# A transformer block on one core: another chain in its opening, three unread products instead of four, and one tensor for what a k-tile reads

## The chip, the core and the metric

The kernel runs on one core of one Trainium2 chip. Its engines work side by side: TensorE (PE) multiplies, with weight loads (PEld) that overlap its products; VectorE (DVE) and ScalarE (ACT) do elementwise work; GpSimd (POOL) and SyncE (SP) issue DMAs here, which 16 DMA engines carry out. The metric is the time of one execution in microseconds of the device (us).

## The reference

One block with 256 tokens of width 1024, all in float32. A vector c gives six modulation vectors; the tokens are scaled and shifted by two of them and multiplied by w_in. The opening of the kernel, which the change touches, computes this:

```
mod = jax.nn.silu(c) @ w_ada[l] + b_ada[l]
sh1, sc1, g1, sh2, sc2, g2 = jnp.split(mod[:, None, :], N_MOD, axis=-1)
h = x * (1.0 + sc1) + sh1
y = token_mixer(h, w_in[l], ...)          # begins with proj = h @ w_in
x = layer_norm(DEEPNORM_ALPHA * x + g1 * y, ln1_g[l], ln1_b[l])
...
y = conv_ffn(h, ...)
x = layer_norm(DEEPNORM_ALPHA * x + g2 * y, ln2_g[l], ln2_b[l])
```

The mixer is attention and a retention branch with gates; conv_ffn is a gated feed-forward layer with a convolution over three tokens. Both come after the opening and stay as they are.

## The kernel before

Products are made with split numbers: a float32 operand becomes a high part (a rounded copy that ACT writes) and a low part (the difference, which DVE writes), and three products stand for one: high by high, high by low, low by high. The helper `split` (L65 to L67) makes both parts, `mm3` (L80 to L83) the three products. ACT writes `whi` and DVE `wlo` for weights, `hh` and `hl` for tokens.

The opening works on eight k-tiles of 128 rows of the inner dimension, in an order written out by hand in `SEQ` (L34). For tile j:

- `a j`, in `h1(j, 0)` (L161): the load of ada tile j is read. DVE multiplies it with the row `srow` (silu of c, spread over all partitions by transposes on PE, L133 to L144) and sums along the row: two instructions of L153, one for the scale and one for the shift, and L170 adds the bias. This gives the modulation `mod` of tile j as two columns.
- `W j`, in `halves_A` (L181): the tile of 2048 columns of w_in is split in two halves of 1024. Behind the first piece of the first half the function `mid` is called, which is `h1(j, 1)`: ACT makes `h32`, the modulated tokens, from the transposed tokens `xT` with mod as scale and bias (L174); for j from 1 up `split` makes `hh` (a copy of h32) and `hl`. For j = 0 DVE makes `hh` straight from xT (L189), and ACT's h32 serves `hl` alone. Pieces are 512 wide in tile 0 (`j < CHUNK`).
- `P j`, in `products_A` (L196): 24 products of 512 columns into eight PSUM banks. In tile 0 they come in the order high by high for both token blocks, high by low for both, low by high for both (L204); in the others as three of `mm3` for each token block, so that `hl` is read by the third product.
- `X`/`Q` are two further weight tiles between them, for a gate.

Before the first real product PE executes `BUSY` products whose result nothing reads (L146 to L148), each on the first 512 columns of ada tile 0.

Loads are issued by SP in order (L70 to L75), into four buffers of 1 MB (`RAW_BUFS`); `load_A` (L114) issues the next of the list when a buffer has been read: for a weight tile first the tokens xT (128 KB) and then the weights (1 MB). `PIECES` says in how many pieces along the columns a tile is loaded: ada tile 0 in three, weight tiles 0 to 3 in four each, all others whole. In the instruction order a load waits for the completion of the load eight before it, and for the readers of its buffer. Ada tiles, tokens and weight tiles lie in three tensors, ada1, xT and winA, with rows of 8 KB, 1 KB and 8 KB, each k-tile a block without gaps.

After the opening the stream of the other weights and PE's products run on in an order fixed by the program; that code is not touched.

Of the kernel before, what the change touches and what calls it, by code (L numbers as in the profile page):

```python
# [9 lines left out]
AF = mybir.ActivationFunctionType  # L10
OP = mybir.AluOpType
# [16 lines left out]
CONST_AT, FIRST = 1, 2  # L28
T0_AT, XN, PRIME = 4, 256, 3
W0, W1, W2 = (4, 5), (6,), (7,)  # L30
PIECES = dict(ada1=[(0, 512, 1024, 2048)] + [1] * 7, winA=[4] * 4 + [1] * 4, winX=[1] * 2)
CHUNK = 1
BUSY = 4
SEQ = [(s[0], int(s[1])) for s in  # L34
       ("a0 W0 P0 a1 W1 P1 a2 W2 P2 a3 W3 P3 X0 Q0 a4 X1 W4 Q1 P4 a5 W5 P5 a6 W6 P6 a7 W7 P7").split()]

# [15 lines left out]
def _body(nc, a, out, pe, act, dve, sp, cst, wts, big, tmp, ps, dram):  # L52
    f = lambda ap: ap.bitcast(F32)
# [4 lines left out]
    def slot(n, shape, dt=F32):  # L58
        return big.tile(shape, dt, tag=f"A{n}", name=f"A{n}")
# [5 lines left out]
    def split(hi, lo, src):  # L65
        act.activation(hi, src, AF.Copy)  # L66
        dve.tensor_tensor(lo, src, f(hi), OP.subtract)  # L67


    def load_raw(src, pieces=1):  # L70
        t = wts.tile([128, 2048], F32, tag="raw", name="raw", bufs=RAW_BUFS)
        cuts = range(0, 2049, 2048 // pieces) if isinstance(pieces, int) else pieces
        for c0, c1 in zip(cuts, cuts[1:]):
            sp.dma_start(t[:, c0:c1], src[:, c0:c1])  # L74
        return t  # L75

    def new_hl():
        return [wts.tile([128, 1024], F32R, tag=n, name=n, bufs=HL_BUFS) for n in ("whi", "wlo")]

    def mm3(o, lh, ll, rh, rl, start, stop):  # L80
        pe.matmul(o, lh, rh, start=start, stop=False)  # L81
        pe.matmul(o, lh, rl, start=False, stop=False)  # L82
        pe.matmul(o, ll, rh, start=False, stop=stop)  # L83
# [19 lines left out]
    mod = cst.tile([128, 6, 8], F32, name="mod")  # L103

    raws = {}
# [8 lines left out]
    def load_A():  # L114
        if not loads_A:
            return
        name, j = loads_A.pop(0)
        if name == "winA":
            raws["xT", j] = slot(("3a", "3b", "6a", "6b")[j % 4], [128, 256])
            sp.dma_start(raws["xT", j], a["xT"][j])  # L120
        raws[name, j] = load_raw(a[name][j], PIECES[name][j])

    for _ in range(RAW_BUFS):
        load_A()
# [20 lines left out]

    for i in range(BUSY):  # L146
        raw = raws["ada1", 0]
        pe.matmul(bank(5), raw[:, i * 128:i * 128 + 128], raw[:, :512], start=True, stop=True)  # L148

    def ada(raw, sec, j, rows=slice(0, 1024)):  # L150

        junk = tmp.tile([128, 1024], mybir.dt.bfloat16, name="junk", bufs=1)
        dve.tensor_tensor_reduce(out=junk[:, rows], in0=raw[:, rows], in1=srow[:, rows], scale=1.0, scalar=0.0,  # L153
                                 op0=OP.mult, op1=OP.add, accum_out=mod[:, sec, j:j + 1])


    hh = slot(0, [128, 8, 256], F32R)
    hl = slot(1, [128, 8, 256], F32R)
    pa = [bank(i) for i in range(8)]

    def h1(j, part):  # L161

        if part == 0:
            ra = raws.pop(("ada1", j))
            if j == 0:
                ada(ra, 0, 0, slice(0, 512))
                dve.tensor_tensor(bcol[:, 0, 0:1], bcol[:, 0, 0:1], mod[:, 0, 0:1], OP.add)
            for i in range(2):
                ada(ra[:, i * 1024:(i + 1) * 1024], i, j, slice(512 if i == j == 0 else 0, 1024))
            dve.tensor_tensor(mod[:, 0:2, j], mod[:, 0:2, j], bcol[:, 0:2, j], OP.add)  # L170
            load_A()
        else:
            h32 = slot(("7a", "7b")[j % 2], [128, 256])
            act.activation(h32, raws.pop(("xT", j)), AF.Identity, scale=mod[:, 0, j:j + 1],  # L174
                           bias=mod[:, 1, j:j + 1])
            if j:
                split(hh[:, j], hl[:, j], h32)
            else:
                dve.tensor_tensor(hl[:, j], h32, f(hh[:, j]), OP.subtract)

    def halves_A(name, j, mid=lambda: None):  # L181
        rw = raws.pop((name, j))
        for half in range(2):
            hi, lo = whl[name, j, half] = new_hl()
            w = 512 if name == "winA" and j < CHUNK else 1024
            for c in range(0, 1024, w):
                if name == "winA" and j == half == c == 0:

                    dve.tensor_scalar(hh[:, 0], raws["xT", 0], mod[:, 0, 0:1], mod[:, 1, 0:1],  # L189
                                      op0=OP.mult, op1=OP.add)  # L190
                split(hi[:, c:c + w], lo[:, c:c + w], rw[:, half * 1024 + c:half * 1024 + c + w])
                if half == c == 0:
                    mid()
        load_A()

    def products_A(j):  # L196
        for half in range(2):
            hi, lo = whl.pop(("winA", j, half))
            for c in range(2):
                if j == 0:  # L200
                    cs = slice(c * 512, (c + 1) * 512)
                    for i, (x, w) in enumerate(((hh, hi), (hh, lo), (hl, hi))):
                        for t in range(2):
                            pe.matmul(pa[half * 4 + c * 2 + t], x[:, j, t * 128:(t + 1) * 128], w[:, cs],  # L204
                                      start=i == 0, stop=False)
                    continue
                for t in range(2):
                    mm3(pa[half * 4 + c * 2 + t], hh[:, j, t * 128:(t + 1) * 128],
                        hl[:, j, t * 128:(t + 1) * 128], hi[:, c * 512:(c + 1) * 512],
                        lo[:, c * 512:(c + 1) * 512], j == 0 or j == 4 and half == 0,  # L210
                        j == 7 or j == 3 and half == 0)
# [18 lines left out]
    for do, j in SEQ:  # L230
        if do == "a":
            h1(j, 0)
        elif do == "W":
            halves_A("winA", j, lambda: h1(j, 1))
        elif do == "X":
            halves_A("winX", j)
        elif do == "P":
            products_A(j)
            if j == 3:
                for i in range(4):  # L240
                    act.activation(qk[i % 2][:, i // 2 * 512:i // 2 * 512 + 512], pa[i], AF.Copy)
        else:
            products_X(j)
            if j == 1:
                for i in range(4):
                    act.activation(ga[:, 2 * i:2 * i + 2].rearrange("p a b -> p (a b)"), pa[i], AF.Copy)
# [941 lines left out]
```

## Time and profile before

| what | us |
|---|---|
| median of 3 runs (lowest, highest) | 439.35 (437.95, 439.85) |
| the profiled execution's own time | 437.57 |
| its span, first to last instruction | 435.8 |
| PE busy in the span | 423.9 |
| DVE busy | 346.0 |
| ACT busy | 240.9 |

The span is what the trace covers; the execution's time has a little around it. All runs are executions of the same program. Matmuls are pipelined, so a busy PE is not PE at its peak. "Landing" is the moment at which a load is complete; rows of the load queue give the time of issue, and another view the time from issue to landing. A row of the timeline gives start, length, engine, line, operation, what it writes and reads, and in brackets the idle time ahead of it and what ended it.

### The profile page before, as it was taken

To read this page: it belongs to the slowest core of one execution; us is meant where nothing else is said; L and a number is where in the kernel's file an instruction comes from. 1 tells how busy PE (TensorE), PEld (TensorE's weight loads), DVE (VectorE), ACT (ScalarE), POOL (GpSimd) and SP (SyncE) were. 2 spreads that over 40 slices of the span, in tenths; PEclk is the share of its full clock that TensorE was granted. 3 is DMA by queue.
4 is the path that set the end of the run, shared out by engine and by line. 5 is a ranking of instruction groups with operands and counts; after the bars stand their busy time and mean duration, and the time that the engine had idled before them with its cause. 6 is when DMAs were issued, how large, how long until landed. Compare 5 with 4: busy or idle time off the path is not lost.

```text
span 435.8 us, 6920 instructions
## 1 busy us (share of the span) xinstructions
PE 423.9 (97%) x2740; PEld 379.6 (87%) x2740; DVE 346.0 (79%) x548; ACT 240.9 (55%) x367; POOL 6.7 (2%) x16
## 2 busy tenths in 40 slices
PE   6999999999999999999999999999999999999993
PEld 3778888877788999999989899899999999999882
DVE  4878689969997999698779887798886665576476
ACT  4466568579774478543443995655445545355500
POOL 0000000100000000000000010000000000000000
PEclk9999999999999999999999999999999999999998
DMA  7999897786568878779562079576666774550001
GB/s 246 413 418 368 321 341 280 303 338 232 168 277 290 289 290 295 280 290 335 211 270 110 0 250 412 174 265 265 277 237 246 291 273 163 194 192 2 2 24 72
DMA packets 19840, 105.72 MB, mean 243 GB/s; under 512 B 2528, under 2 KB 4576, under 8 KB 8544
## 3 DMA queue, kind: packets, MB, share of 16 engines
q1 hardware_dynamic: 18432, 100.29, 61.4%
q0 software_dynamic: 1376, 4.99, 3.3%
q8 instruction: 21, 0.34, 0.3%
q14 instruction: 11, 0.09, 0.1%
HBM read 104.22 MB, written 1.06 MB: 242 GB/s over the span
## 4 chain that ended last, share of the span: by engine, by line
PE 92%; DVE 3%; DMA 2%; ACT 1%; SPq 1%; issue 0%; DVEq 0%
PE P L81 28%; PE P L82 28%; PE P L83 28%; DMA raw<-in_ada 2%; DVE junk L153 2%; PE P L532 1%; PE P L534 1%; PE P L535 1%; PE P L776 1%; PE P L828 1%; PE P L847 1%; SPq L74 1%; PE P L871 1%; DVE wlo L67 1%; ACT whi L66 0%; PE P L917 0%
## 5 line engine op out<-in xcount | busy, mean ns | idle before, releaser
L1042 DVE TENSOR_TENSOR wlo<-raw,whi 128x1024 fp32r<-128x1024 f32 x118 | 140.4, 1219 | 24.7 <-ACT whi L1028 24.7
L1028 ACT ACTIVATE whi<-raw 128x1024 fp32r<-128x1024 f32 x118 | 120.1, 1051 | 39.6 <-PE P L83 16.0
L83 PE MATMUL P<-whi,A 128*128 128x512 f32 (+1 forms) x220 | 83.3, 379 | 0.0
L81 PE MATMUL P<-whi,A 128*128 128x512 f32 (+1 forms) x176 | 68.7, 390 | 1.1 <-ACT A L66 1.1
L82 PE MATMUL P<-wlo,A 128*128 128x512 f32 (+1 forms) x176 | 66.9, 380 | 0.0
L153 DVE CUSTOM_DVE_ANT_0 junk<-raw,srow 128x1024 bf16<-128x1024 f32 (+1 forms) x49 | 58.7, 1197 | 3.9 <-DMA raw<-in_ada 1.8
L81 PE MATMUL P<-A3a,whi 128*128 128x256 f32 x192 | 54.4, 283 | 0.0
L81 PE MATMUL P<-A3b,whi 128*128 128x256 f32 x192 | 54.3, 283 | 0.0
L82 PE MATMUL P<-A6b,whi 128*128 128x256 f32 x192 | 54.3, 283 | 0.0
L83 PE MATMUL P<-A3b,wlo 128*128 128x256 f32 x192 | 54.3, 283 | 0.0
L83 PE MATMUL P<-A3a,wlo 128*128 128x256 f32 x192 | 54.3, 283 | 0.0
L82 PE MATMUL P<-A6a,whi 128*128 128x256 f32 x192 | 54.3, 283 | 0.0
L83 PEld LDWEIGHTS P<-whi,A 128*128 128x128 f32 x220 | 41.4, 188 | 8.3 <-DVE A L67 0.3
L81 PE MATMUL P<-A,whi 128*128 128x256 f32 x160 | 45.9, 287 | 0.0
L83 PE MATMUL P<-A,wlo 128*128 128x256 f32 x160 | 45.2, 283 | 0.0
L82 PE MATMUL P<-A,whi 128*128 128x256 f32 x160 | 45.2, 283 | 0.0
L81 PEld LDWEIGHTS P<-whi,A 128*128 128x128 f32 x176 | 33.1, 188 | 9.2 <-ACT A L66 2.3
L82 PEld LDWEIGHTS P<-wlo,A 128*128 128x128 f32 x176 | 33.1, 188 | 5.8
L82 PEld LDWEIGHTS P<-A6a,whi 128*128 128x128 f32 x192 | 36.8, 192 | 0.3
L81 PEld LDWEIGHTS P<-A3a,whi 128*128 128x128 f32 x192 | 36.8, 192 | 0.3
L81 PEld LDWEIGHTS P<-A3b,whi 128*128 128x128 f32 x192 | 36.9, 192 | 0.0
L82 PEld LDWEIGHTS P<-A6b,whi 128*128 128x128 f32 x192 | 36.9, 192 | 0.0
(234 smaller groups left out, 724.0 us busy)
## 6 DMA issues: line engine op xcount, KB each, us to landing
raw<-in_ada SPq DMA_DIRECT2D x23, 1024.0 KB, 5.8
raw<-in_wup SPq DMA_DIRECT2D x11, 1024.0 KB, 4.8
raw<-in_wgate SPq DMA_DIRECT2D x11, 1024.0 KB, 5.2
raw<-in_wdown SPq DMA_DIRECT2D x11, 1024.0 KB, 4.9
raw<-in_winB SPq DMA_DIRECT2D x10, 1024.0 KB, 5.7
raw<-in_winA SPq DMA_DIRECT2D x16, 256.0 KB, 6.6
raw<-in_winA SPq DMA_DIRECT2D x4, 1024.0 KB, 5.8
raw<-in_winGr SPq DMA_DIRECT2D x4, 1024.0 KB, 5.7
```

What stands on the lines that cost most here:

```text
L67: dve.tensor_tensor(lo, src, f(hi), OP.subtract)
L74: sp.dma_start(t[:, c0:c1], src[:, c0:c1])
L81: pe.matmul(o, lh, rh, start=start, stop=False)
L82: pe.matmul(o, lh, rl, start=False, stop=False)
L83: pe.matmul(o, ll, rh, start=False, stop=stop)
L153: dve.tensor_tensor_reduce(out=junk[:, rows], in0=raw[:, rows], in1=srow[:, rows], scale=1.0, scalar=0.0, op0=OP.mult, op1=OP.add, accum_o ...
L532: pe.matmul(p, xl(k)[:, tk], hi[:, c], start=False, stop=k == 7)
L534: pe.matmul(p, xh(k)[:, tk], hi[:, c], start=k == 0, stop=False)
L535: pe.matmul(p, xh(k)[:, tk], lo[:, c], start=False, stop=False)
L776: pe.transpose(p[:, i * 128:(i + 1) * 128], roped[:, which * 512 + i * 128:which * 512 + (i + 1) * 128], ident)
L1028: act.activation(hi, src, AF.Copy)
L1042: dve.tensor_tensor(lo, src, f(hi), OP.subtract)
```

## The change

- `BUSY` goes from 4 to 3.
- `CHUNK` goes from 1 to 2: tile 1, too, is split in pieces of 512 columns, with the product order of tile 0. In tile 1 `mid` is called behind the second piece of the first half (`mid_at`).
- For tiles from 1 up ACT writes `hh` straight from xT with scale and bias, and then h32 in the same way; the copy from h32 is gone. DVE's `hl` is the difference as before.
- Pieces: ada tiles 1 to 3 in two each instead of whole; weight tiles 2 and 3 in two instead of four.
- The tensors ada1, xT and winA become one, `strm`: in each of its 8 times 128 rows lie 2048 columns of ada, 256 of tokens and 2048 of weights, 17 KB together. The loads read column ranges of it.

```diff
-PIECES = dict(ada1=[(0, 512, 1024, 2048)] + [1] * 7, winA=[4] * 4 + [1] * 4, winX=[1] * 2)
-CHUNK = 1
-BUSY = 4
+PIECES = dict(ada1=[(0, 512, 1024, 2048)] + [2] * 3 + [1] * 4, winA=[4] * 2 + [2] * 2 + [1] * 4, winX=[1] * 2)
+CHUNK = 2
+BUSY = 3
...
-            sp.dma_start(raws["xT", j], a["xT"][j])
-        raws[name, j] = load_raw(a[name][j], PIECES[name][j])
+            sp.dma_start(raws["xT", j], a["strm"][j][:, 2048:2304])
+        src = {"ada1": a["strm"][:, :, :2048], "winA": a["strm"][:, :, 2304:], "winX": a["winX"]}[name][j]
+        raws[name, j] = load_raw(src, PIECES[name][j])
...
-            act.activation(h32, raws.pop(("xT", j)), AF.Identity, scale=mod[:, 0, j:j + 1],
-                           bias=mod[:, 1, j:j + 1])
-            if j:
-                split(hh[:, j], hl[:, j], h32)
-            else:
-                dve.tensor_tensor(hl[:, j], h32, f(hh[:, j]), OP.subtract)
+            for o in (h32,) if j == 0 else (hh[:, j], h32):
+                act.activation(o, raws["xT", j], AF.Identity, scale=mod[:, 0, j:j + 1], bias=mod[:, 1, j:j + 1])
+            raws.pop(("xT", j))
+            dve.tensor_tensor(hl[:, j], h32, f(hh[:, j]), OP.subtract)
...
             w = 512 if name == "winA" and j < CHUNK else 1024
+            mid_at = 512 if 0 < j < CHUNK else 0
...
-                if half == c == 0:
+                if half == 0 and c == mid_at:
                     mid()
...
-                if j == 0:
+                if j < CHUNK:
...
-                                      start=i == 0, stop=False)
+                                      start=i == j == 0, stop=False)
...
-        xT=x.T.reshape(8, 128, 256),
-        ada1=np.concatenate([colsT(1), colsT(0)], 2),
+        strm=np.concatenate([colsT(1), colsT(0), x.T.reshape(8, 128, 256), wi[:, :2048].reshape(8, 128, 2048)], 2),
...
-        winA=wi[:, :2048].reshape(8, 128, 2048),
```

## The prediction, made before the changed kernel ran

> **What bounds the kernel now.** I read the page first, then the windows by stage, then the chain of waits, then the timeline of the first 30 us.
>
> ```profile
> span 435.8 us, 6920 instructions
> PE 92%; DVE 3%; DMA 2%; ACT 1%; SPq 1%; issue 0%; DVEq 0%
> ```
>
> The span is 435.8 us, the profiled execution's own time 437.57, so 1.8 us lie around the span. The chain that ends last is PE for 92%: what is gained elsewhere counts only if PE gets its work sooner.
>
> ```profile
> core 0: us, PE busy (x) PEld busy (x) DVE busy (x) ACT busy (x) POOL busy (x), PEclk, DMA share, GB/s
> 5.00:10.50 5.50, 5.33 (x9) 1.32 (x9) 4.08 (x11) 2.07 (x4) 0.00 (x0) 1.00 1.00 312
> 10.50:17.46 6.96, 6.08 (x26) 4.51 (x24) 5.72 (x10) 3.40 (x7) 0.00 (x0) 1.00 1.03 418
> 17.46:23.30 5.84, 5.83 (x24) 4.42 (x24) 5.40 (x9) 2.96 (x5) 0.00 (x0) 1.00 1.03 410
> 23.30:28.80 5.50, 5.49 (x25) 4.36 (x24) 4.91 (x9) 2.63 (x4) 0.00 (x0) 1.00 1.05 420
> 60.00:100.00 40.00, 40.00 (x193) 32.40 (x192) 35.86 (x61) 29.78 (x49) 1.22 (x2) 1.00 0.78 294
> ```
>
> From 60 us on PE has no idle time, so an edit of the opening can only move the start of that unbroken stretch. In the opening PE, DVE and the 16 DMA engines are all nearly full: DMA share 1.00 to 1.05. But the same share moves 312 GB/s in 5.00:10.50 and 410 to 420 afterwards. The chain of waits shows what PE waits for there:
>
> ```profile
> 5.11 8.49 DMA raw<-in_ada
> 13.63 1.22 DVE junk L153
> 14.90 1.23 DVE junk L153
> 16.36 0.61 ACT A7b L174
> ...
> 18.40 1.23 DVE wlo L67
> 19.62 1.14 DVE junk L153
> ...
> 22.27 0.61 ACT A7a L174
> ...
> 23.23 1.05 ACT whi L66
> ...
> 28.17 0.61 ACT A7b L174
> 28.80 0.43 ACT A L66
> 29.27 0.50 PE P L81
> ```
>
> Up to 29.27 us the chain does not run over PE but over the modulation weights: the load of ada tile 1 lands at 5.11 + 8.49 = 13.60, DVE reduces its two halves, ACT makes the modulated tokens, and so on for tiles 2 and 3. After 29.27 it is PE. So the figure to forecast is how much earlier PE's tile 3 starts and proceeds.
>
> **The unread products (BUSY 4 to 3).**
>
> ```profile
> 8.78 0.30 PEld L148 LDWEIGHTS P<-raw 128*128 128x128 f32 x2 [1.43 <-PE P L148]
> 9.96 0.30 PEld L148 LDWEIGHTS P<-raw 128*128 128x128 f32 x2 [0.89 <-PE P L148]
> 9.03 0.63 ACT L66 ACTIVATE whi<-raw 128x512 fp32r<-128x512 f32 x1 [3.30 <-DMA raw<-in_winA]
> 15.96 0.61 PE L204 MATMUL P<-whi,A 128*128 128x512 f32 x2
> 14.60 1.07 PE L204 MATMUL P<-whi,A 128*128 128x512 f32 x4
> 15.51 0.62 PE L204 MATMUL P<-wlo,A 128*128 128x512 f32 x2
> ```
>
> The third unread product begins at 8.78 and the fourth at 9.96: 1.18 us apart. The first high part of weight tile 0 is ready at 9.03 + 0.63 = 9.66, so without the fourth product PE can begin its real work at about 9.96, and all of tile 0 moves 1.1 us ahead (its end from 15.96 + 0.61 = 16.57 to about 15.5). Its 24 products run at (15.51 - 14.60) / 4 = 0.23 us each; high and low parts come in time. By itself this is worth nothing, because tile 1 is not ready at 16.57 either (next part): PE would wait 1.1 us longer.
>
> The Trainium skill speaks against this cut: "TensorE: Matmul & The Clock Gate", section "Part 1: The HAM clock gate", says that the array runs at half rate until a free-running window of some 3.4 us has been busy. Here the third unread product already runs at the full pace, so the trace does not show a real product at half rate; by the page a later window would put some five of tile 0's products at half rate, about 1 us, which the wait before tile 1 covers, so the sum by it is the same.
>
> **Tile 1: ada in two pieces, weights in halves of 512.**
>
> ```profile
> 10.70 1.89 DVE L67 TENSOR_TENSOR wlo<-raw,whi 128x512 fp32r<-128x512 f32 x3
> 15.37 1.06 ACT L66 ACTIVATE whi<-raw 128x1024 fp32r<-128x1024 f32 x1 [3.52 <-DMA raw<-in_winA]
> 10.05 1.80 ACT L66 ACTIVATE whi<-raw 128x512 fp32r<-128x512 f32 x3
> 17.46 0.50 PE L81 MATMUL P<-whi,A 128*128 128x512 f32 x1 [0.89 <-ACT A L66]
> 20.84 1.06 ACT L66 ACTIVATE whi<-raw 128x1024 fp32r<-128x1024 f32 x1 [2.48 <-DMA raw<-in_winA]
> ```
>
> With two pieces the first reduction needs only the first half of the tile, which lands 524 KB / 418 GB/s = 1.25 us before 13.60, at 12.35. DVE is free at 10.70 + 1.89 = 12.59 and does the two at the pace of the rows (14.90 - 13.63 = 1.27): 12.6, 13.9, modulation ready at 15.3 instead of 16.3, 1.0 earlier. What is late next is the weight: its second 512 columns land at 15.37. ACT then needs 0.60 for that high part and 0.60 for the tokens (the 16.36 row of the chain): PE starts at about 16.6 instead of 17.46, 0.85 earlier. The price is two more ACT and two more DVE instructions: four of 0.60 (1.80 / 3) for two of 1.06, 0.3 us of ACT, covered by its waits of 3.52 and 2.48 us.
>
> Only part of this 0.85 reaches tile 2. Its ada lands where it did (19.03, below), and DVE, which began at 19.6, can begin there: about 0.45 earlier, modulation 2 at 21.8.
>
> **The order of the token tiles (j from 1 up).** Before, ACT made h32 and copied it to hh; now it makes hh first and h32 second, both with scale and bias. hh is ready one copy (0.42) earlier; h32, from which hl follows, is later by one Identity less the copy's place.
>
> ```profile
> 9.56 0.58 ACT L174 ACTIVATE A7a<-A3a,mod 128x256 f32<-128x256 f32 x1
> 23.35 0.42 DVE L67 TENSOR_TENSOR A<-A7a,A 128x256 fp32r<-128x256 f32 x1
> 23.83 0.19 PEld L83 LDWEIGHTS P<-whi,A 128*128 128x128 f32 x1 [0.16 <-DVE A L67]
> 29.25 0.42 DVE L67 TENSOR_TENSOR A<-A7b,A 128x256 fp32r<-128x256 f32 x1
> ```
>
> ACT's next instruction after the 9.56 one began at 10.05, so an Identity occupies 0.49. hl follows 2 x 0.49 + 0.1 + 0.42 = 1.5 after the first begins; before, 23.35 + 0.42 - 22.27 = 1.5 too. So hl, which the third product of tiles 2 and 3 reads, gains nothing from the new order, and PE will wait there for some 0.4 us (it starts earlier and waits at hl instead: the 0.16 wait grows). In tile 1 it does not, because there the new product order reads hl fifth. So tiles 2 and 3 keep only the DVE chain's gain: modulation 3 comes 0.4 earlier (ACT's second weight half begins 0.4 earlier than 23.23, the low part and two reductions follow), hl begins at 28.9 instead of 29.25 and is there at 29.3. Before, PE read it only at 29.27 + 0.57 = 29.84 (two products after a late first one), so PE's tile 3 is **0.5 us** ahead, with landings as before. The seven longer ACT instructions (0.60 for 0.42) cost 1.3 us of an engine with waits on every tile.
>
> **Loads.** One issue less in all (three ada tiles +1 each, two weight tiles -2 each). Ada tiles 1 to 3 go from 8 KB to 4 KB rows, weight tiles 2 and 3 from 2 KB to 4 KB. In the instruction order each load waits for the one eight before it, so tile 1's tokens go out not at 5.60 but when the last piece of ada tile 0 has landed, for which DVE waits until 7.38: up to 1.8 us later. The pieces still have 5 us in the queue:
>
> ```profile
> 5.60 0.47 SPq L120 DMA_DIRECT2D A3b<-in_xT  x1
> 7.38 1.22 DVE L153 CUSTOM_DVE_ANT_0 junk<-raw,srow 128x1024 bf16<-128x1024 f32 x1 [0.75 <-DMA raw<-in_ada]
> 7.26 2.73 SPq L74 DMA_DIRECT2D raw<-in_winA x4
> raw<-in_winA SPq DMA_DIRECT2D x1, 256.0 KB, 7.4
> 11.12 0.33 SPq L74 DMA_DIRECT2D raw<-in_ada x1
> raw<-in_ada SPq DMA_DIRECT2D x1, 1024.0 KB, 7.9
> ```
>
> The 7.26 piece lands at 14.66 and ada tile 2 at 11.12 + 7.9 = 19.0, behind a full queue. I cost the issues at nothing; with the queue empty they would cost their lateness, 1.8 us.
>
> The one tensor changes addresses alone: rows of a k-tile lie 17 KB apart instead of 8, and tokens 1 KB in 17. The trace shows no such load. Upper bound of a gain: had 5.00:10.50 run at the 418 of the next stretch, its 1,716 KB would have taken 4.1 us, **1.4** less, and everything that waits for a landing comes that much sooner. Lower bound of a gain: 0, the same start-up. Bound of a loss: the whole opening stays at 312; the 7,613 KB of 10.50:28.80 then take 24.4 instead of 18.3 us, **6.1** more. I take a gain of **1.0**: the next stretch carries 2 KB pieces too (ada and weights of tiles 1 and 2) at 418, so the low rate belongs to the start and not to the piece size, and the addresses are what the change alters in that start. That is a choice, nearer to the upper end.
>
> Sum: 0.5 from the chain + 1.0 from the landings = 1.5 us. 437.57 - 1.5 = 436.1 for an execution like the profiled one; the runs' median, 439.35, lies 1.8 above it, so the forecast is **437.85**. Ceiling: PE from 9.96 with three tiles of about 5.55 us and no gap begins tile 3 at 26.6, 2.6 ahead.
>
> **Rivals.**
> 1. *The landings stay.* The queue's start-up is the same for any address. For it: the sizes and the first eight issues are unchanged. Gain 0.5: 438.85.
> 2. *The low start rate is the spacing's, all of it.* Equal rows 8 KB apart make 16 engines that start in step meet in the same memory; 17 KB rows don't. For it: 312 against 418 at the same share. Against: later tiles have the same spacing and run at 418. All landings 1.4 to 2 earlier bring PE to its ceiling: 2.5 less, 436.85. The Trainium skill, "DMA: Bandwidth & Descriptors", section "Latency and other measured facts", tells of such slow row pitches, cured by a few KiB of padding, but for pitches from 512 KiB up; no run here shows it.
> 3. *The wide rows read slower.* Whole 1 MB blocks become 128 separate rows in 2.2 MB. The opening's loads, without slack, set PE's start; each 1% of 18.3 us is 0.18, so 3% less rate eats the 0.5 and 15% passes the measurable loss. At 312 throughout: 6.1 - 0.5 = 5.6 more, 445; I would expect about +3, 442. Against: 2 KB pieces at 8 KB distance already run at 418.
> 4. *The change of order doesn't do what it says*: hl waits take back the 0.5 of rival 1. Then 439.3.
>
> **How the numbers follow.** Forecast 0.34, rival 1 0.16, rival 2 0.30, rival 3 0.15, rival 4 0.05. 0.5% (2.2 us: below 437.15, above 441.55) is about what a measurement of this kernel can tell from no change. Faster: rival 2's larger part 0.27 and the forecast's edge 0.07, 0.34. Slower: 0.14 of rival 3. Same: 0.52. The forecast's own range is 437.0 to 438.7; the range that holds 8 in 10 reaches to rival 2's time with the runs' scatter of some 1 us below, and to the beginning of rival 3 above: 435.6 to 441.5.
>
> **What would show it.** Chain: the first L204 product near 9.9; modulation 1 ready near 15.3 or, with faster landings, 14.3; first product of tile 1 near 16.6 (15.6); waits of the third product (L83) of tiles 2 and 3 on DVE of about 0.4 us. Loads: GB/s in 5.00:10.50 above 312, ada tile 1's second piece landing before 13.6. Tile 3's first L81 product near 27.3 to 28.5, and no idle PE behind it. Wrong, if the GB/s of 10.5 to 28.8 fall below 400, if PE goes idle after tile 3, or if the shift at 60 us differs from that of tile 3.

## The result, and the profile after

| | before | changed |
|---|---|---|
| median, us (10 runs each) | 438.35 (437.95 to 439.85) | 437.23 (436.9 to 438.08) |
| ratio of times | 1 | 0.9967, 95% interval 0.9956 to 0.9978 |
| profiled execution, us | 437.57 | 437.32 |
| span, us | 435.8 | 435.5 |

The changed kernel is faster by 0.33% (438.35 x 0.0033 = 1.45 us; the medians differ by 1.12). Measured once more (e9 below) it had the ratio 0.998 (0.9971 to 0.9989), 0.9 us. The profiled execution of before, at 437.57, was quicker than each of these ten runs, so the two traces alone differ by only 0.3 us.

The page of the changed kernel, its span and the chain's shares by engine:

```profile
span 435.5 us, 6921 instructions
PE 92%; DMA 4%; DVE 2%; issue 1%; ACT 0%; SPq 0%; DVEq 0%
```

The windows by stage of the changed kernel, with the columns as before:

```profile
5.00:10.50 5.50, 4.25 (x9) 1.17 (x8) 3.86 (x11) 2.17 (x4) 0.00 (x0) 1.00 1.01 352
10.50:17.46 6.96, 6.49 (x29) 4.87 (x28) 6.50 (x14) 4.11 (x9) 0.00 (x0) 1.00 1.04 409
17.46:23.30 5.84, 5.50 (x23) 3.91 (x22) 5.30 (x9) 3.09 (x5) 0.00 (x0) 1.00 1.03 417
23.30:28.80 5.50, 5.50 (x24) 4.24 (x23) 4.79 (x7) 2.66 (x5) 0.00 (x0) 1.00 1.04 434
60.00:100.00 40.00, 40.00 (x193) 32.39 (x192) 36.10 (x61) 30.29 (x50) 1.22 (x2) 1.00 0.76 295
```

The loads' start is quicker, 352 GB/s against 312, and later stages are not slower. Still the share is full at a rate below 409: most of the start's loss stays. The chain of waits of the changed kernel:

```profile
2.10 5.85 DMA raw<-in_strm
7.97 5.94 DMA A3b<-in_strm
13.98 6.60 DMA raw<-in_strm
20.62 0.94 issue
21.57 0.58 ACT A L176
...
23.62 0.72 DVE wlo L67
24.77 1.22 DVE junk L154
26.03 1.22 DVE junk L154
27.33 0.45 issue
27.78 1.24 DVE wlo L67
29.06 0.50 PE P L82
```

Up to 20.6 the chain now consists of loads: DVE's reductions of tiles 1 and 2 are off it. The tokens of tile 1 go out at 7.97, when the last piece of ada tile 0 has landed (2.10 + 5.85), and when they have landed (7.97 + 5.94 = 13.91) the load eight places behind goes out, at 13.98. Behind that come the low parts of the weights and the reductions of tile 3, up to the second product (L82) of tile 3. The timeline of the changed kernel has the moments that the prediction named:

```profile
10.08 0.30 PEld L204 LDWEIGHTS P<-whi,A 128*128 128x128 f32 x2 [1.93 <-ACT whi L66]
12.62 1.22 DVE L154 CUSTOM_DVE_ANT_0 junk<-raw,srow 128x1024 bf16<-128x1024 f32 x1
13.88 1.23 DVE L154 CUSTOM_DVE_ANT_0 junk<-raw,srow 128x1024 bf16<-128x1024 f32 x1
15.15 0.16 DVE L171 TENSOR_TENSOR mod<-mod,first 128x2 f32<-128x2 f32 x1
15.73 0.59 ACT L176 ACTIVATE A<-A3b,mod 128x256 fp32r<-128x256 f32 x1
16.36 0.30 PEld L204 LDWEIGHTS P<-whi,A 128*128 128x128 f32 x2 [0.89 <-ACT A L176]
22.20 0.19 PEld L81 LDWEIGHTS P<-whi,A 128*128 128x128 f32 x1 [0.49 <-ACT A L176]
22.97 0.19 PEld L82 LDWEIGHTS P<-wlo,A 128*128 128x128 f32 x1 [0.58 <-DVE wlo L67]
29.05 0.19 PEld L82 LDWEIGHTS P<-wlo,A 128*128 128x128 f32 x1 [0.66 <-DVE wlo L67]
29.40 0.49 PE L83 MATMUL P<-whi,A 128*128 128x512 f32 x1
```

Tile 0 begins at 10.1, modulation 1 is ready at 15.15 + 0.16 = 15.3, tile 1 begins at 16.4. In tiles 2 and 3 PE waits at the second product, for the low part of the weights. The third product of tile 3 stands at 29.40; before, and behind it the first product after tile 3, before and after:

```profile
29.84 0.39 PE L83 MATMUL P<-whi,A 128*128 128x512 f32 x1
34.94 1.03 PE L218 MATMUL P<-A10a 1*128 1x512 bf16 x4
34.61 1.03 PE L218 MATMUL P<-A10a 1*128 1x512 bf16 x4
```

The third product is 0.44 us earlier in these two traces, the product behind tile 3 0.33, and from there both traces take 400.9 us to their ends: what tile 3 has gained is what the span has gained. In this execution the second half of ada tile 1 landed at 6.18 + 7.4 = 13.6 us (issue and time to landing), no sooner than the whole tile before (13.60). So these two traces show mostly the chain's part of the gain; an earlier landing is to be seen in e9.

### The profile page after: what moved, and what is told of

It reads as the page before. It is cut to its first block, busy times and chain, and to the rows that moved or that the text cites. A ratio compares the mean times of both kernels' runs of the same rounds, so it can differ in the third digit from the quotient of the medians.

```text
span 435.5 us, 6921 instructions
## 1 busy us (share of the span) xinstructions
PE 422.5 (97%) x2738; PEld 379.0 (87%) x2738; DVE 346.1 (79%) x550; ACT 241.7 (55%) x369; POOL 6.7 (2%) x16
## 4 chain that ended last, share of the span: by engine, by line
PE 92%; DMA 4%; DVE 2%; issue 1%; ACT 0%; SPq 0%; DVEq 0%
PE P L81 28%; PE P L82 28%; PE P L83 28%; DMA raw<-in_strm 3%; DMA A3b<-in_strm 1%; PE P L532 1%; PE P L534 1%; PE P L535 1%; PE P L776 1%; PE P L828 1%; PE P L847 1%; PE P L871 1%; DVE junk L154 1%; DVE wlo L67 0%; PE P L917 0%
## 5 line engine op out<-in xcount | busy, mean ns | idle before, releaser
L83 PE MATMUL P<-whi,A 128*128 128x512 f32 (+1 forms) x212 | 80.3, 379 | 0.0
L81 PE MATMUL P<-whi,A 128*128 128x512 f32 (+1 forms) x168 | 65.4, 389 | 0.1
L82 PE MATMUL P<-wlo,A 128*128 128x512 f32 (+1 forms) x168 | 64.0, 381 | 0.5 <-DVE wlo L67 0.5
L82 PE MATMUL P<-A6b,whi 128*128 128x256 f32 x192 | 54.3, 283 | 0.0
L82 PE MATMUL P<-A6a,whi 128*128 128x256 f32 x192 | 54.3, 283 | 0.0
L83 PEld LDWEIGHTS P<-whi,A 128*128 128x128 f32 x212 | 39.9, 188 | 7.9
L82 PE MATMUL P<-A,whi 128*128 128x256 f32 x160 | 45.2, 283 | 0.0
L81 PEld LDWEIGHTS P<-whi,A 128*128 128x128 f32 x168 | 31.6, 188 | 7.1 <-issue 1.3
L82 PEld LDWEIGHTS P<-wlo,A 128*128 128x128 f32 x168 | 31.7, 188 | 6.7 <-DVE wlo L67 1.2
L82 PEld LDWEIGHTS P<-A6a,whi 128*128 128x128 f32 x192 | 36.8, 192 | 0.3
L82 PEld LDWEIGHTS P<-A6b,whi 128*128 128x128 f32 x192 | 36.9, 192 | 0.0
```

## The experiments

All were timed against the kernel before on the same chip, with medians of before of 438.19 (e1 to e4), 438.68 (e5 to e8) and 438.02 us (e9 to e12). The first two groups ran on one chip, and still the kernel before differs by 0.5 us between them, so medians are compared within a group only. "Chain", "clock" and "landing" are the three theories: the gain comes from tile 1's pieces and the reductions; from fewer unread products; from the one tensor.

| run | what | ratio to before (95% interval) | median, us |
|---|---|---|---|
| e1 | before, three unread products | 1.0007 (0.9994 to 1.0021) | 438.45 |
| e2 | before, six unread products | 1.0018 (1.0004 to 1.0031) | 438.67 |
| e3 | before, one tensor | 0.9992 (0.9983 to 1.0001) | 437.64 |
| e4 | changed, three tensors | 0.9987 (0.9974 to 1.0000) | 437.67 |
| e5 | changed, four unread products | 0.9976 (0.9964 to 0.9989) | 437.27 |
| e6 | changed, high part copied from h32 | 0.9967 (0.9956 to 0.9979) | 437.25 |
| e7 | changed, tile 1 like tiles 2 and 3 | 0.9979 (0.9966 to 0.9992) | 437.61 |
| e8 | changed, other order of products in tiles 2 and 3 | 0.9953 (0.9937 to 0.9969) | 436.39 |
| e9 | the changed kernel again | 0.9980 (0.9971 to 0.9989) | 437.14 |
| e10 | changed, three tensors, rows 17 KB apart | 0.9981 (0.9972 to 0.9991) | 437.24 |
| e11 | changed, one tensor, rows 8 KB apart | 0.9990 (0.9980 to 0.9999) | 437.62 |
| e12 | changed, three tensors, rows 8 KB apart (as e4) | 0.9994 (0.9982 to 1.0006) | 437.73 |

**e1, e2: the unread products alone.**

```diff
-BUSY = 4
+BUSY = 3        # e1; e2: BUSY = 6
```

> The kernel before with three unread products instead of four, nothing else. Chain theory (the gain comes from tile 1's pieces; the fourth unread product is covered by the wait ahead of tile 1): ratio 1.000 within 0.001, and tile 1 still begins near 17.4 us. Clock theory (in most executions PE reaches full pace later than in the profiled one, so four unread products push tile 0 into tile 1's time): ratio 0.998 or less, 0.8 us or more. Landing theory (the one tensor brings the gain): 1.000.

> The kernel before with six unread products. Each more costs 1.2 us at full pace (the fourth in the trace: 9.96 to 11.1); tile 0 then ends at 16.6 + 2.3 = 18.9. Chain theory: 1.4 us of it show behind tile 1's old start at 17.46, less 0.3 us of later gaps: ratio about 1.0025. Clock theory: more, two further products at half rate in part of the executions, ratio 1.004 or more. Landing theory says nothing of it.

Cutting one gives nothing (1.0007), and two more cost 0.0018, less than two of 1.2 us each would on the path: chain holds, clock in the form stated falls. But the trace of e1 shows a third thing, in its weight loads, its windows and its products:

```profile
17.51 0.19 PEld L81 LDWEIGHTS P<-whi,A 128*128 128x128 f32 x1 [2.71 <-ACT A L66]
```

```profile
18.20:21.60 3.40, 3.40 (x10) 2.64 (x10) 3.12 (x4) 0.72 (x2) 0.00 (x0) 0.51 1.03 396
21.60:25.00 3.40, 3.40 (x16) 2.81 (x15) 2.84 (x6) 2.52 (x4) 0.00 (x0) 0.99 1.00 401
```

```profile
17.52 0.50 PE L81 MATMUL P<-whi,A 128*128 128x512 f32 x1 [2.28 <-ACT A L66]
...
18.59 0.63 PE L81 MATMUL P<-whi,A 128*128 128x512 f32 x1
19.01 0.63 PE L82 MATMUL P<-wlo,A 128*128 128x512 f32 x1
19.44 0.63 PE L83 MATMUL P<-whi,A 128*128 128x512 f32 x1
...
24.84 0.39 PE L81 MATMUL P<-whi,A 128*128 128x512 f32 x1
```

Tile 0 ended 1.3 us sooner (its last products begin at 14.62 instead of 15.96) and PE then stood idle for 2.3 to 2.7 us; from 18.2 to 21.6 the granted clock is 0.51 and products start 0.42 apart instead of 0.23. Tile 1 took 24.84 - 17.52 = 7.3 us instead of the 5.9 before. So the fourth unread product was covered, but in that kernel its removal lengthens a wait that can cost the clock: 1.4 us on this tile. How often, the granted clock of the single runs tells as far as a mean over the whole run can: 3.4 us at 0.51 take 3.4 x 0.49 / 436.7 = 0.004 from it, and the trace of e1 has 0.990, the thirteen others 0.994 to 0.997. It was 0.991 or less in 4 of e1's 12 runs, in 3 of the 100 runs of the kernel before in the three groups, and in no run of the other kernels. The eight other runs of e1 have the median 438.34, next to the 438.19 of the kernel before. The Trainium skill, "TensorE: Matmul & The Clock Gate", section "Part 1: The HAM clock gate", gives such a fall back to half rate after an idle window of some 3.4 us. The half-rate stretch here lasted 3.4 us, but the idle time ahead of it, 2.3 to 2.7 us, was shorter than the Trainium skill's figure. That the idle time brought the fall is inferred: no run varies this wait alone.

**e3, e4: the one tensor alone, and the rest alone.** The edit of the loads and of the host arrays from the diff above, put into the kernel before (e3) and taken out of the changed one (e4).

```diff
+            sp.dma_start(raws["xT", j], a["strm"][j][:, 2048:2304])       # e3
+        src = {"ada1": a["strm"][:, :, :2048], "winA": a["strm"][:, :, 2304:], "winX": a["winX"]}[name][j]
...
+            sp.dma_start(raws["xT", j], a["xT"][j])                       # e4
+        raws[name, j] = load_raw(a[name][j], PIECES[name][j])
```

> The kernel before with ada, tokens and weights of a k-tile in one row of one tensor, pieces and everything else as before. Landing theory: ratio 0.9975 (1 us), more GB/s in 5.00:10.50 than 312, ada tile 1 landed before 13.0. Chain and clock theories: 1.000 within 0.001.

> The changed kernel with the old three tensors, all else changed. Landing theory: the gain of 1.45 us falls to 0.5, ratio 0.999. Chain and clock theories: the gain stays, ratio 0.997.

Neither theory holds alone: the tensor by itself brings 0.0008, the rest by itself 0.0013, each interval touching 1. The 0.0033 of the changed kernel came from another comparison, so the two parts needed one in common (e9 and e12 below). In e3's trace the load of ada tile 1 landed at 5.23 + 7.7 = 12.9 us, with 363 GB/s in 5.00:10.50, as landing theory had it; the time did not follow. A possible reason lies far behind the opening. e3's timeline:

```profile
81.27 1.06 ACT L1029 ACTIVATE whi<-raw 128x1024 fp32r<-128x1024 f32 x1 [5.23 <-DMA raw<-in_winB]
83.19 0.60 ACT L779 ACTIVATE A3a<-P 128x512 f32<-128x512 f32 x1
83.84 1.14 PE L777 MATMUL P<-first,A2b 128*128 128x128 f32 x8 [0.57 <-ACT A3a L779]
```

and the same ACT instruction in the kernel before:

```profile
80.36 1.06 ACT L1028 ACTIVATE whi<-raw 128x1024 fp32r<-128x1024 f32 x1 [3.64 <-PE P L83]
```

In e3 ACT waits for a weight load until 81.27; behind it in ACT's order stand the copies that empty two PSUM banks (L779), and PE's next transposes need those banks. PE's stretch from the product behind tile 3 to the end took 436.0 - 34.26 = 401.7 us instead of 400.9: 0.8 us of what the opening had won was given back. Why that load came late is not shown. e11's trace has the same wait (0.64 at the same place; 436.1 - 34.30 = 401.8). In e12 that stretch took 401.2, and in the other traces 400.9 to 401.0.

**e5, e6, e7: one edit of the changed kernel undone.**

```diff
-BUSY = 3
+BUSY = 4                                    # e5
...
-            for o in (h32,) if j == 0 else (hh[:, j], h32):      # e6
-                act.activation(o, raws["xT", j], AF.Identity, scale=mod[:, 0, j:j + 1], bias=mod[:, 1, j:j + 1])
+            act.activation(h32, raws.pop(("xT", j)), AF.Identity, scale=mod[:, 0, j:j + 1],
+                           bias=mod[:, 1, j:j + 1])
+            if j:
+                split(hh[:, j], hl[:, j], h32)
+            else:
+                dve.tensor_tensor(hl[:, j], h32, f(hh[:, j]), OP.subtract)
...
-CHUNK = 2
+CHUNK = 1                                   # e7
```

> The changed kernel with four unread products. Chain theory: tile 0 then ends near 16.4, before tile 1 is ready at 16.4, so ratio as the changed kernel's, 0.997. Clock theory: 0.8 us or more are lost, 0.9985 or more.

> The changed kernel with the old way to the token tiles (ACT makes h32 first and copies it to the high part; the low part as before). My step says that the low part comes no later or sooner by the order, so tiles 2 and 3 lose nothing and tile 1 begins 0.3 to 0.4 us later, which tile 2's wait covers: ratio as the changed kernel's within 0.0005. Rival: the high part's earlier start is worth 0.4 us: ratio higher by 0.001.

> The changed kernel with tile 1 handled like tiles 2 and 3 (splits of 1024 columns, low part of the tokens read by the third product). Chain theory: tile 1 starts later by up to 0.4 us and waits 0.4 us at its third product, DVE's next tile begins 0.3 us later: ratio higher than the changed kernel's by 0.0007. If tile 1's pieces do nothing: the same ratio.

e6 has the best ratio of the three and the one first measured for the changed kernel: the new way to the token tiles is worth nothing that can be seen, as expected, though the changed kernel itself was not in this group and its two ratios, 0.9967 and 0.998, differ by more than the 0.0005 of the expectation. In what follows e6 stands in for it. Against e6, tile 1 without its pieces loses 0.0012 (0.5 us by the ratios; by the means of the twelve runs each 0.29, with a 95% interval from -0.1 to 0.7; expected 0.3), and a fourth unread product 0.0009 (0.4 us by the ratios, nothing by medians or means). The intervals of the three overlap, so neither loss is shown.

The pieces of tile 1 have a price that no step named. The low part for tile 3 begins in the changed kernel, and then in e7:

```profile
27.78 1.23 DVE L67 TENSOR_TENSOR wlo<-raw,whi 128x1024 fp32r<-128x1024 f32 x1 [0.32 <-issue]
27.56 1.22 DVE L67 TENSOR_TENSOR wlo<-raw,whi 128x1024 fp32r<-128x1024 f32 x1
```

All nine traces with tile 1 in pieces have this idle time of 0.32 to 0.34 us on DVE, just ahead of the low part for which PE's second product of tile 3 waits; the five without pieces have none, e7 among them, which differs in the pieces alone. Its cause is not known.

**e8: the waits of tiles 2 and 3 filled.**

```diff
+                if j in (2, 3) and half == 0:
+                    if c == 0:
+                        for i, (x, w) in enumerate(((hh, hi), (hh, lo), (hl, hi))):
+                            for cc in range(2):
+                                for t in range(2):
+                                    pe.matmul(pa[cc * 2 + t], x[:, j, t * 128:(t + 1) * 128],
+                                              w[:, cc * 512:(cc + 1) * 512], start=False,
+                                              stop=j == 3 and i == 2)
+                    continue
```

> The changed kernel with another order of products in the first half of tiles 2 and 3: four high by high, then four high by low, then four low by high, so that the waits before the second product (0.77 and 0.63 us from start to start in the changed kernel's trace, against 0.34 without a wait) are filled with products that are ready. Expected: 0.3 us less, ratio lower by 0.0007 than the changed kernel's. Rival: the work is only moved, the next wait takes it: the same ratio.

It has the lowest median of all twelve, 0.86 us below e6 and 2.3 below the kernel before on that chip. Its weight loads:

```profile
21.20 0.76 PEld L212 LDWEIGHTS P<-whi,A 128*128 128x128 f32 x4 [0.40 <-ACT A L176]
27.14 0.76 PEld L212 LDWEIGHTS P<-whi,A 128*128 128x128 f32 x4 [0.63 <-ACT A L176]
28.07 0.76 PEld L212 LDWEIGHTS P<-wlo,A 128*128 128x128 f32 x4 [0.17 <-DVE wlo L67]
```

The waits on wlo of 0.58 and 0.66 have shrunk to none and 0.17. From the start of tile 2 to the product behind tile 3 it takes 32.85 - 21.20 = 11.65 us, the changed kernel 34.61 - 22.20 = 12.41: 0.76 less. That is not the 0.3 expected but about all of the two waits, (0.77 - 0.34) + (0.63 - 0.34) = 0.72. The rest of this execution's lead was a quick start of its loads (380 GB/s in 5.00:10.50). Against e6 the intervals of the ratios overlap, but the single runs of the two part: e8's nine took 0.87 us less in the mean than e6's twelve, with a 95% interval of about 0.4 to 1.3.

**e9 to e12: spacing or neighbourhood.** Four kernels that differ in the layout alone: one tensor or three, rows 17 KB or 8 KB apart.

```diff
-        strm=np.concatenate([colsT(1), colsT(0), x.T.reshape(8, 128, 256), wi[:, :2048].reshape(8, 128, 2048)], 2),
+        **{n: np.concatenate([colsT(1), colsT(0), x.T.reshape(8, 128, 256), wi[:, :2048].reshape(8, 128, 2048)], 2)
+           for n in ("xT", "ada1", "winA")},                                          # e10
...
+        strm=np.concatenate([np.concatenate([colsT(1), colsT(0)], 2), x.T.reshape(8, 16, 2048),
+                             wi[:, :2048].reshape(8, 128, 2048)], 1),                  # e11
```

> The changed kernel itself (one tensor, rows 17 KB apart), for comparison with the next three on the same chip: ratio 0.997.

> The changed kernel with ada, tokens and weights in three tensors again, but each with rows 17 KB apart, so that every load's addresses are spaced as in the changed kernel. Spacing theory (8 KB between the rows of a load slows its start): as the changed kernel, 0.997, ada tile 1 complete near 13.0. Neighbourhood theory (what counts is that a k-tile's loads lie together in one tensor): as with three tensors of 8 KB rows, 0.9985, ada tile 1 complete near 13.5.

> The changed kernel with one tensor in which each k-tile's ada, tokens and weights follow each other as blocks without gaps, rows 8 KB (tokens 1 KB) apart as before. Spacing theory: 0.9985, ada tile 1 complete near 13.5. Neighbourhood theory: 0.997, near 13.0.

> The changed kernel with the old three tensors again (8 KB rows, tokens 1 KB), on the same chip as the three others: both theories 0.9985, ada tile 1 complete near 13.5; if it has the changed kernel's ratio, the one tensor is worth nothing and the difference seen before was the chips'.

The ratios pair by spacing: 0.9980 and 0.9981 with 17 KB, 0.9990 and 0.9994 with 8 KB, whether in one tensor or in three. Each is 0.0005 to 0.001 above its expectation, and taken singly their intervals overlap. Together, each run counted by itself, the 23 runs with 8 KB took 0.53 us longer in the mean than the 22 with 17 KB, with a 95% interval of about 0.2 to 0.9; between one tensor and three the difference is 0.1, and its interval has zero inside. The traces, in the order e9, e10, e11, e12, first the window of the loads' start (one fence for each kernel), then the start of tile 1 among the weight loads (for e9 with the end of tile 1's modulation ahead of it):

```profile
5.00:10.50 5.50, 5.38 (x10) 1.67 (x10) 4.87 (x13) 3.13 (x6) 0.00 (x0) 1.00 1.02 376
```

```profile
5.00:10.50 5.50, 4.72 (x12) 1.58 (x11) 4.49 (x12) 2.89 (x6) 0.00 (x0) 1.00 1.00 370
```

```profile
5.00:10.50 5.50, 4.96 (x10) 1.46 (x10) 4.32 (x11) 2.27 (x5) 0.00 (x0) 1.00 0.98 349
```

```profile
5.00:10.50 5.50, 5.38 (x12) 2.10 (x12) 4.65 (x12) 2.80 (x5) 0.00 (x0) 1.00 1.00 351
```

```profile
14.20 0.16 DVE L171 TENSOR_TENSOR mod<-mod,first 128x2 f32<-128x2 f32 x1
15.63 0.30 PEld L204 LDWEIGHTS P<-whi,A 128*128 128x128 f32 x2 [0.40 <-ACT A L176]
```

```profile
15.46 0.30 PEld L204 LDWEIGHTS P<-whi,A 128*128 128x128 f32 x2 [0.69 <-ACT A L176]
```

```profile
16.07 0.30 PEld L204 LDWEIGHTS P<-whi,A 128*128 128x128 f32 x2 [0.96 <-ACT A L176]
```

```profile
16.03 0.30 PEld L203 LDWEIGHTS P<-whi,A 128*128 128x128 f32 x2 [1.32 <-ACT A L175]
```

With 17 KB the start moves 370 and 376 GB/s and tile 1 begins at 15.5 and 15.6; with 8 KB 349 and 351 GB/s, and 16.0 and 16.1. The second half of ada tile 1 landed at 12.8 (5.63 + 7.2) and 12.6 (5.71 + 6.9) with 17 KB, at 13.3 (6.17 + 7.1) and 13.2 (5.82 + 7.4) with 8 KB. Spacing theory holds. (The tokens' rows lie 1 KB apart in the kernels called 8 KB.) It is a trend over executions: the rate of the profiled one of the changed kernel was 352. Over all fourteen traces the window has 340 to 380 GB/s with 17 KB (eight traces) and 312 to 351 with 8 KB (six).

## Why the prediction was right, and where its steps failed

The forecast was a gain of 1.5 us, 0.5 from the chain and 1.0 from the landings. Measured: 1.45 us by the ratio of the first comparison, 0.9 by that of e9. The direction was right, the traces show both sources, and the gain stays inside the 0.5% that the prediction named as its likeliest case. That the first comparison met the sum within 0.05 is in part luck: measured again the gain was 0.9, and its parts measured singly are about 0.4 and 0.35 to 0.6. The forecast time, 437.85 against 437.23, stands on a median of three runs, 439.35; ten runs have 438.35, from which the same 1.5 would have given 436.85.

- *Only the start of the unbroken stretch moves.* Right in eleven of the fourteen traces (400.9 to 401.0 us from the product behind tile 3 to the end). Wrong in e3 and e11, where PE stood 0.6 us at 83 us and 0.8 or more was lost, and in part in e12 (401.2). The prediction named the idle time of PE behind tile 3 as what would prove it wrong and did not look for a place where it could arise.
- *The fourth unread product is covered.* Right in time (e1). The step missed that the longer wait can take the clock away (e1's 0.51): the Trainium skill's rule was weighed for a late rise to the full rate only, not for a fall. In the changed kernel itself PE waits 1.9 us ahead of tile 0 and 0.9 ahead of tile 1, and the clock stays at 1.00.
- *Tile 0 near 9.96.* 10.1 in the changed kernel's trace: ada tile 0's last piece landed late, DVE wrote the first high part of the tokens from 9.55 to 9.96, and PE waited 1.93 us. There the unread products did not bind. In e9 that part was written by 8.94, PE was at its third unread product from 9.02 and began tile 0 at 9.6, so there they did.
- *Tile 1.* Modulation ready at 15.3 as worked out; first product 16.4 instead of 16.6. e9 shows the other case that the prediction named, with faster landings: modulation ready at 14.20 + 0.16 = 14.4 (14.3 forecast), first product 15.6 (15.6). What the pieces are worth at the end is not shown: 0.3 to 0.5 us, within the noise (e7). DVE's idle 0.3 us ahead of tile 3, which comes with them, is a price that the step did not have.
- *The issues, costed at nothing.* The tokens of tile 1 went out at 7.97 instead of 5.60, 2.4 us later where up to 1.8 had been worked out, and the chain of the changed kernel passes through their landing. Still ACT's first high part of weight tile 2, at the end of that chain, begins at 20.60, before it was 20.84: no loss shows.
- *Tiles 2 and 3.* The size was right, the place of the wait wrong. It was put at the third product, for hl; it is at the second, for the low part of the weights, which stands ahead of hl in DVE's order: 0.77 us from the first product to the second instead of 0.34. So the new order of the token tiles gains nothing (e6), as the step said, for another reason. e8 shows what the waits cost: 0.76 us.
- *The chain's 0.5.* e4 and e12, the changed kernel without the layout: 0.0013 and 0.0006, 0.57 and 0.26 us, mean 0.4. Both intervals reach 1. The 0.44 us of the third product of tile 3 speak for the size, as ada tile 1 landed no sooner there, though the weights of tile 2 did by 0.2.
- *The landings' 1.0.* Mis-sized by the choice near the upper bound: e9 against e12 0.0014 or 0.6 us, e3 0.35. The row spacing takes part of the start's loss away, not most of it: 312 to 351 became 340 to 380, and 418 was the bound.
- Rival 1 (landings unchanged) and rival 2 (all of the start's loss) are the two sides of that size; neither came about. What rival 2 gives as its reason, rows that meet in the memory, is not shown; only the spacing's effect is. Rival 3 (17 KB rows read slower) is refuted by e9 and e10, and its 10.5 to 28.8 rates by 409 to 434 GB/s. Rival 4 (hl takes the chain's gain back) is not excluded by the times of e4 and e12, but the trace speaks against it: the wait at hl is gone and the third product is 0.44 us earlier.

What stays open: why the start's loads are slow at all, and why wider spacing helps, as only two spacings were run; why DVE idles 0.3 us before the low part at 27.78, for which the chain names no releaser ("issue"); and what the other number of pieces per load does by itself, which no run undoes.

## What to carry to other kernels

In an opening that waits for loads, order products so that those whose operands come last run last: e8's nine lines brought another 0.86 us by the medians. Reducing and rounding as each piece lands brought the modulation of tile 1 forward by 1.0 us, but no gain at the end that stands clear of the noise (e7). Filler work that looks covered may still hold the clock up; before taking it out, look how long the engine will then be idle. A gain at the start can be lost to one late load far behind it: e3 and e11 lost 0.8 and 0.9 us so.

## What the runs showed that I had not expected

- A wait of 2.3 to 2.7 us on PE was followed by 3.4 us at a granted clock of 0.51 (e1), 1.4 us lost on one tile of 24 products; by the granted clock of the runs in some 4 of 12 executions, against 3 of 100 with one more unread product.
- The spacing of a load's rows in memory matters even at a few KB: 17 KB apart against 8 KB, 19 to 27 GB/s more from 5.0 to 10.5 us with the same sizes (e9 and e10 against e11 and e12), and nothing later.
- One late weight load behind the opening stops PE over ACT's order: ACT waited 5.23 us for it in e3, and the copies behind it kept two PSUM banks occupied.
